# One step of a hybrid attention layer: the high parts of raw weights copied by GpSimd instead of VectorE

## The chip, the cores and the metric

The kernel runs on one core of one Trainium2 chip. A core has five engines with queues of their own, each working in order: TensorE (PE in the profile, its weight loads PEld), VectorE (DVE), ScalarE (ACT), GpSimd (POOL) and SyncE (SP), which here issues all DMAs. The metric is the device time of one execution in microseconds (us). The 1% of this time is about 12 us.

## The reference, cut to what matters

The layer projects a prompt of 2048 tokens (and 8 sample tokens) of width 1024, runs two kinds of attention over it, gates the outputs and projects them back:

```python
h = einsum('bsd,de->bse', x, w_in)
qa, ka, va, ga, qb, kb, vb, gb = split(h)          # rotary on qa, ka, qb, kb
oa = merge of three banded attentions of 8 heads (dilations 1, 4, 16)
ob = banded attention of 8 heads on 2 KV heads, with a learned sink per head
mix = concatenate([oa * silu(ga), ob * silu(gb)])
y = layer_norm(2**0.25 * x + einsum('bse,ed->bsd', mix, w_o))
```

Everything is float32 at the interface.

## The kernel before, in words

A float32 product with accuracy near float32 is made of three products in the faster type float32r: every operand is split into a **high part** (the value rounded to float32r) and a **low part** (value minus high part), and high x high, high x low and low x high are accumulated (`products`, and the same pattern at lines 629 and 672). So every weight tile needs two preparations after its load: a copy into the high part and a subtraction for the low part.

The kernel has three stages. In the first (up to about 381 us of the profile) the K and the A-side Q projections and V are made. In the last (from about 1059 us) the output projection and the normalisation run. Between them lies the steady stage: a loop over 66 steps of attention (`scores`, `weights`, `turn`, `values`; 12 steps for each pair of A heads, then 4 for each pair of B heads), in which TensorE also does the later projections. Those come from a generator (`stream`, `out_weights`) that is advanced by a budget of 3480 ns per step, each of its 256-column products counting n/2.4 ns. In this stage the order of the instructions on every engine is that of the program (a manual schedule): nothing is reordered.

The later projections go in three passes over eight chunks of tokens: QB0, QB1, QB2, G0 in the first pass, G1 to G4 in the second, G5 to G7 in the third. All weights of a pass are replaced at the change to the next: the tiles gw0, gw1 (shown as gw), gw2 and gw3 are reopened as the last chunk has used them. TensorE's products of a projection are shown as pg at line 629.

How these weights arrive is the part around the change. `Parts` puts four raw chunks of a weight (128 x 256 float32 each) into the queue `raws`. At every tick of the loop (four per step) `raw_step` does two things. It takes up to two chunks from the head of the queue whose load was issued at least three ticks ago and whose destination is open, and issues for each a copy into the high part h (line 137) and a subtraction into the low part l on GpSimd (line 138). Then it issues up to two loads (line 142, on SP) into the four buffers named raw. A buffer is free again when the subtraction has read it. 17 weights take this way, 68 chunks: two of the first pass (the other two were prepared before), four of the second, three of the third, and the eight blocks of the output weights (shown as wo, wo6h, wo7h and wl).

Other work on the same queues: on VectorE the mask and row minimum of the scores (line 831, sm), the copies of transposed probabilities out of PSUM (line 859, pT), the regrouping of queries (line 800, qo), the transposed statistics (line 930, stT) and the gates (line 172, th); TensorE's transposes (line 853, ps_pt) and scores (line 823, ps_s) wait for these. On GpSimd the weighting of the three A patterns (`merge_a`, lines 1050 to 1053), whose factors F come by DMA, and the merges of the B pairs (line 990). `merge_a` fetches F two chunks ahead on SP (line 1038), and a fetch waits for the buffer that GpSimd still reads.

Of the kernel before, what the change touches and what calls it, by code (L numbers as in the profile page):

```python
# [51 lines left out]
def hymba_step(ctx, tc, xt, xs, xr, wq, wv, wo, tab, msk, ident, diag, sinks, lng, lnb,  # L52
               kca, vca, kcb, vcb, y, kto, vo):
    nc = tc.nc
    V, S, G, T = nc.vector, nc.scalar, nc.gpsimd, nc.tensor
# [37 lines left out]
    def tick(last=False):  # L93
        slot[0] += 1
        raw_step()
        while due and (last or any(d.at <= slot[0] for d in due)):
            now = [d for d in due if last or d.at <= slot[0]]
            due[:] = [d for d in due if d not in now]
            for d in now:
                d.run()  # L100
# [13 lines left out]
    class Parts:  # L114
# [9 lines left out]
        def __iter__(self):  # L124
            while self.left:
                raw_step(True)
            return iter(self.hl)

    def raw_step(now=False):

        for r in raws:
            r[4] += r[3] is not None
        for _ in range(2):
            if raws and raws[0][0].hl and raws[0][3] is not None and (now or raws[0][4] >= 3):
                p, _, k0, w, _ = raws.popleft()
                h, l = p.hl
                V.tensor_copy(h[:, k0:k0 + 2], w)
                G.tensor_sub(l[:, k0:k0 + 2], w, h[:, k0:k0 + 2].bitcast(F32))
                p.left -= 1
        for r in [r for r in islice(raws, RAW) if r[3] is None][:2]:  # L140
            r[3] = at.tile([128, 2, 128], F32, name="raw", bufs=RAW)
            dma(r[3], r[1][:, r[2]:r[2] + 2])
# [1193 lines left out]
```

## Time and profile before

| what | value |
|---|---|
| median of 3 runs | 1244.24 us (1241.34 to 1249.01) |
| profiled execution | 1243.91 us, span 1242.1 us |
| mean granted TensorE clock | 0.978 of full |
| PE busy | 1149.4 us (93%) |
| DVE busy | 566.0 us (46%) |
| ACT busy | 430.9 us (35%) |
| POOL busy | 328.6 us (26%) |
| DMA | 230.15 MB, mean 185 GB/s |

In rows of the timeline the columns are start in us, duration in us, engine, line of the kernel, operation, output <- inputs, shapes, count; in brackets stands how long the engine was idle just before and what ended that. In rows of a line or tile the numbers behind the count are the shortest, median and longest duration in ns, then the first and last start. In rows of groups they are the busy time and the mean duration, then the idle time just before and its releasers. In rows of waits stand the total in us and the number of times. "EVENT_SEMAPHORE" and the names with a q are the sequencers. A merged row covers several instructions.

### The profile page before, as it was taken

To read this page: it belongs to the slowest core of one execution; us is meant where nothing else is said; L and a number is where in the kernel's file an instruction comes from. 1 tells how busy PE (TensorE), PEld (TensorE's weight loads), DVE (VectorE), ACT (ScalarE), POOL (GpSimd) and SP (SyncE) were. 2 spreads that over 40 slices of the span, in tenths; PEclk is the share of its full clock that TensorE was granted. 3 is DMA by queue.
4 is the path that set the end of the run, shared out by engine and by line. 5 is a ranking of instruction groups with operands and counts; after the bars stand their busy time and mean duration, and the time that the engine had idled before them with its cause. 6 is when DMAs were issued, how large, how long until landed. Compare 5 with 4: busy or idle time off the path is not lost.

```text
span 1242.1 us, 23436 instructions
## 1 busy us (share of the span) xinstructions
PE 1149.4 (93%) x8614; PEld 1006.3 (81%) x8614; DVE 566.0 (46%) x1855; ACT 430.9 (35%) x1417; POOL 328.6 (26%) x402
## 2 busy tenths in 40 slices
PE   8999999999998999995999899779899896999997
PEld 7899999979977888984887788668777774688885
DVE  6432001010023565553666546465666774685434
ACT  3200111101103565552555445435554451133221
POOL 2243112120012000045105302540243323175432
PEclk9999999999999999997999999989999997999998
DMA  8745887283686573677466746854896847655621
GB/s 276 240 134 177 256 277 254 81 272 128 213 259 192 180 188 124 156 187 170 143 153 176 217 144 172 199 147 142 204 226 197 273 145 219 180 168 185 199 94 68
DMA packets 206067, 230.15 MB, mean 185 GB/s; under 512 B 34640, under 2 KB 174576, under 8 KB 205568
## 3 DMA queue, kind: packets, MB, share of 16 engines
q1 hardware_dynamic: 205952, 228.66, 63.2%
q8 instruction: 67, 1.10, 0.4%
q14 instruction: 48, 0.39, 0.1%
HBM read 158.52 MB, written 70.07 MB: 184 GB/s over the span
## 4 chain that ended last, share of the span: by engine, by line
PE 65%; DMA 13%; DVE 7%; ACT 5%; issue 4%; POOL 3%; SPq 2%; POOLq 0%; DVEq 0%; ACTq 0%
PE po L672 13%; PE pg L629 11%; PE ps_s L823 7%; PE pv L527 7%; PE ps_pt L853 5%; PE pmm L152 5%; PE ps L152 5%; PE ppt L152 4%; ACT pe L834 4%; PE ps_o L874 4%; DMA F<-fd 4%; PE po L152 3%; DVE pT L859 3%; DVE sm L831 2%; DMA k<-ks 2%
## 5 line engine op out<-in xcount | busy, mean ns | idle before, releaser
L834 ACT ACTIVATE pe<-sm,st 128x256 f32<-128x256 f32 (+1 forms) x512 | 235.6, 461 | 241.4 <-DVE st L831 240.4
L831 DVE CUSTOM_DVE_ANT_0 sm<-ps_s,mk 128x256 f32<-128x256 f32 (+1 forms) x512 | 180.4, 375 | 143.2 <-PE ps_s L823 132.5
L853 PE MATMUL ps_pt<-idt,pe 128*128 128x128 f32 x848 | 140.3, 286 | 48.5 <-DVE pT L859 37.6
L629 PE MATMUL pg<-gx,gw 128*128 128x256 f32 (+1 forms) x1104 | 167.5, 294 | 5.9 <-DMA gx<-xd 2.9
L853 PEld LDWEIGHTS ps_pt<-idt,pe 128*128 128x128 f32 x848 | 90.7, 141 | 73.3 <-DVE pT L859 48.9
L629 PEld LDWEIGHTS pg<-gx,gw 128*128 128x128 f32 x1104 | 142.7, 192 | 7.5 <-DMA gx<-xd 3.5
L859 DVE COPY pT<-ps_pt 128x512 f32<-128x512 f32 x176 | 121.2, 689 | 28.3 <-PE ps_pt L853 26.4
L1050 POOL TENSOR_TENSOR oT<-oT,F 128x256 f32<-128x256 f32 x32 | 23.4, 731 | 347.3 <-ACT pe L834 179.4
L874 PE MATMUL ps_o<-pT,v 128*64 128x128 f32 (+1 forms) x1120 | 106.0, 333 | 0.0
L874 PEld LDWEIGHTS ps_o<-pT,v 128*64 128x64 f32 x1120 | 69.7, 136 | 39.3 <-issue 16.6
L834 ACT ACTIVATION_READ_ACCUMULATOR pe<-sm,st 128x1 f32 x512 | 95.8, 187 | 0.0
L823 PE MATMUL ps_s<-k,qo 64*128 64x256 f32 (+1 forms) x768 | 95.5, 390 | 0.0
L823 PEld LDWEIGHTS ps_s<-k,qo 64*128 64x128 f32 x768 | 69.3, 195 | 13.4 <-issue 1.8
L629 PE MATMUL pg<-gx,gw2h 128*128 128x256 f32 (+1 forms) x368 | 75.1, 292 | 1.2 <-ACT spe L406 1.2
L527 PE MATMUL pv<-wvh,xh 128*128 128x384 f32 (+1 forms) x224 | 69.6, 311 | 0.0
L527 PE MATMUL pv<-wvh,xl 128*128 128x384 f32 (+1 forms) x224 | 69.5, 310 | 0.0
L527 PE MATMUL pv<-wvl,xh 128*128 128x384 f32 (+1 forms) x224 | 69.4, 310 | 0.0
L672 PE MATMUL po<-wl,mho 128*128 128x512 f32 x192 | 59.7, 392 | 0.0
L629 PEld LDWEIGHTS pg<-gx,gw2h 128*128 128x128 f32 x368 | 58.3, 191 | 1.5 <-ACT spe L406 1.5
L629 PE MATMUL pg<-gx,gw2l 128*128 128x256 f32 (+1 forms) x184 | 53.9, 293 | 0.0
L539 ACT ACTIVATE vf<-pv 128x384 f32<-128x384 f32 (+1 forms) x32 | 14.0, 438 | 112.7 <-PE pv L527 62.2
L172 DVE SCALAR_TENSOR_TENSOR th<-th,pg 128x256 f32<-128x256 f32 (+1 forms) x64 | 26.9, 420 | 48.7 <-ACT th L168 48.3
(262 smaller groups left out, 2461.8 us busy)
## 6 DMA issues: line engine op xcount, KB each, us to landing
gx<-xd SPq DMA_DIRECT2D x80, 512.0 KB
F<-fd SPq DMA_DIRECT2D x80, 192.0 KB
gs<-th SPq DMA_DIRECT2D x64, 128.0 KB
v<-vs SPq DMA_DIRECT2D x28, 256.0 KB
xd<-xh SPq DMA_DIRECT2D x12, 512.0 KB
xd<-xl SPq DMA_DIRECT2D x12, 512.0 KB
kc<-in_kca SPq DMA_DIRECT2D x8, 768.0 KB
vc<-in_vca SPq DMA_DIRECT2D x6, 1024.0 KB
```

The lines of the kernel that those rows point to most:

```text
L152: T.matmul(p[:, :n], a[:, kt, :], b, start=k == 0, stop=k == 23)
L172: V.scalar_tensor_tensor(th[:, :n], th[:, :n], 1.0, p, op0=OP.add, op1=OP.mult)
L527: T.matmul(p[:, :w], l, r[:, kt, :w], start=k == 0, stop=k == 23)
L629: T.matmul(p[:, :n], a[:, kt, :], b[:, kt % 2, :n], start=kt + e == 0, stop=kt == 7 and e == 2)
L672: T.matmul(p, a, b[:, nh * 4:nh * 4 + 4].rearrange("p a b -> p (a b)"), start=first and k == 0, stop=last and k == end)
L823: T.matmul(s[:, h, n % 4, :w], self.Q[g][r, n % 4 * 128:n % 4 * 128 + 128], self.keys(n)[r], start=True, stop=True)
L831: V.tensor_tensor_reduce(sm[:, :w], self.s[:, h, n % 4, :w], mk[:, MI[self.d], 256 - w:], -0.125, 3.0e38, op0=OP.add, op1=OP.min, accum_out=m)
L834: S.activation(p[:, :w], sm[:, :w], AF.Exp, scale=-1.0, bias=m, accum_out=den)
L853: T.transpose(pt[:, h, j], self.P[h, n][:, a:a + 128], idt)
L859: V.tensor_copy(t, pt)
L874: T.matmul(o[64 * h:64 * h + 64, a:a + 128 * len(ns)], v[:, cv, kv:kv + 64], t[:, h, j:j + len(ns)].rearrange("p a b -> p (a b)"), start=n ...
L1050: G.tensor_mul(m, m, F[:, 0])
```

## The change

The copy into the high part in `raw_step` is issued on GpSimd instead of VectorE. The subtraction that follows it stays on GpSimd, and so do the loads on SP, the buffers, the order of the queue `raws` and all other code.

```diff
             if raws and raws[0][0].hl and raws[0][3] is not None and (now or raws[0][4] >= 3):
                 p, _, k0, w, _ = raws.popleft()
                 h, l = p.hl
-                V.tensor_copy(h[:, k0:k0 + 2], w)
+                G.tensor_copy(h[:, k0:k0 + 2], w)
                 G.tensor_sub(l[:, k0:k0 + 2], w, h[:, k0:k0 + 2].bitcast(F32))
                 p.left -= 1
```

## The prediction

> **What bounds the kernel now.** I read the page first: the share of each engine, then the chain that ended last.
>
> ```profile
> span 1242.1 us, 23436 instructions
> PE 1149.4 (93%) x8614; PEld 1006.3 (81%) x8614; DVE 566.0 (46%) x1855; ACT 430.9 (35%) x1417; POOL 328.6 (26%) x402
> PE 65%; DMA 13%; DVE 7%; ACT 5%; issue 4%; POOL 3%; SPq 2%; POOLq 0%; DVEq 0%; ACTq 0%
> ```
>
> TensorE bounds the kernel, so only time in which it stands still can be won: 1242.1 - 1149.4 = 93 us. VectorE (DVE) has over half the span free, so relieving it of busy time means little; what counts is where it stands in front of something TensorE needs. So the second view is line 137, the copy that the change moves, and what it waits for.
>
> ```profile
>   DMA raw<-in_wq: 28.6, 8
>   DMA raw<-in_wo: 5.0, 3
>   POOL gw2l L138: 27.2, 5
> ```
>
> VectorE stood 28.6 + 5.0 = 33.6 us waiting for raw weights in eleven places. The third row is the other direction: GpSimd (POOL) waited 27.2 us for copies that VectorE had not reached yet. Third, the timeline shows whether TensorE stood still in these places. The first is the change from the first to the second pass of the projections.
>
> ```profile
> 569.46 1.89 SPq L142 DMA_DIRECT2D raw<-in_wq  x4
> 575.37 1.96 DVE L137 CAST gw<-raw 128x256 fp32r<-128x256 f32 x4 [13.18 <-DMA raw<-in_wq]
> 577.58 1.12 PE L853 MATMUL ps_pt<-idt,pe 128*128 128x128 f32 x4 [10.25 <-DVE stT L930]
> 578.68 2.80 POOL L138 TENSOR_TENSOR gw<-raw,gw 128x256 fp32r<-128x256 f32 x4
> 585.23 0.64 DVE L137 CAST gw<-raw 128x256 fp32r<-128x256 f32 x2 [2.55 <-DMA raw<-in_wq]
> 586.53 0.44 PE L853 MATMUL ps_pt<-idt,pe 128*128 128x128 f32 x2 [2.78 <-DVE pT L859]
> 588.28 3.15 PE L823 MATMUL ps_s<-k,qo 64*128 64x256 f32 x16
> 597.19 0.63 PE L629 MATMUL pg<-gx,gw 128*128 128x256 f32 x4
> 599.71 2.00 PE L823 MATMUL ps_s<-k,qo 64*128 64x256 f32 x16
> ```
>
> VectorE's queue came to the copy at 562.2 us, 7 us before the load was even issued. The attention's copies (stT, then sm and pT) stood behind it, and TensorE behind these: 10.25 and 2.78 us. The weights were not needed yet: the second pass begins at 597.19. The second place is the next change of pass, the third the loads of the output weights before the last stage.
>
> ```profile
> 807.95 0.64 DVE L137 CAST gw<-raw 128x256 fp32r<-128x256 f32 x2 [7.25 <-DMA raw<-in_wq]
> 809.24 1.12 PE L853 MATMUL ps_pt<-idt,pe 128*128 128x128 f32 x4 [7.19 <-DVE pT L859]
> 812.45 1.43 DVE L137 CAST gw<-raw 128x256 fp32r<-128x256 f32 x2 [2.59 <-DMA raw<-in_wq]
> 814.54 0.44 PE L853 MATMUL ps_pt<-idt,pe 128*128 128x128 f32 x2 [2.43 <-DVE pT L859]
> 815.88 3.68 PE L823 MATMUL ps_s<-k,qo 64*128 64x256 f32 x16
> 816.13 2.77 POOL L138 TENSOR_TENSOR gw<-raw,gw 128x256 fp32r<-128x256 f32 x4
> 834.69 1.23 PE L629 MATMUL pg<-gx,gw 128*128 128x264 f32 x8
> ```
>
> ```profile
> 1041.21 0.69 DVE L137 CAST wo7h<-raw 128x256 fp32r<-128x256 f32 x2 [2.45 <-DMA raw<-in_wo]
> 1043.98 0.37 PE L963 MATMUL pst<-idt,wts 128*32 128x128 f32 x1 [4.65 <-DVE wts L959]
> 1080.45 144.14 PE po L672 x622
> ```
>
> The last row is the chain of waits: after these places TensorE runs through, so what is won before arrives at the end.
>
> **The change part by part.** 68 copies (17 weights in four chunks each) go from VectorE to GpSimd, each directly ahead of the subtraction of the same chunk. Loads, their order on SP, buffers and subtractions stay.
>
> *Removed, first change of pass:* TensorE's waits of 10.25 + 2.78 = 13.0 us go. What could be late next: the q and v of the coming steps.
>
> ```profile
> 563.32 1.19 SPq L782 DMA_DIRECT2D v<-vs  x2
> 579.13 1.08 SPq L906 DMA_DIRECT2D q<-qa  x2
> ```
>
> These are the last issues of either. The v is wanted by the values of the step that now begins at 588.28, the q two steps later; with some 6 us to land, neither is late for a TensorE 13 us earlier.
>
> *Removed, second change:* 7.19 + 2.43 = 9.6 us. *Removed, tail:* 4.65 us; the seven small VectorE operations of the merge no longer stand behind wo7h.
>
> *Slow clock behind the stalls.*
>
> ```profile
> 540.00:562.00 22.00, 22.00 (x190) 19.30 (x189) 13.99 (x51) 13.77 (x51) 9.25 (x13) 1.00 0.90 237
> 562.00:578.00 16.00, 5.75 (x49) 4.38 (x48) 2.77 (x9) 0.49 (x2) 8.92 (x14) 0.76 0.84 171
> ```
>
> These are windows before and in the first stall (engines in the order PE, PEld, DVE, ACT, POOL; then the granted clock, 1.00 against 0.76, the DMA engines' share and GB/s). Sixteen scores take 2.00 us at 599.71, but 3.15 at 588.28 and 3.68 at 815.88: 1.15 + 1.68 = 2.8 us. Transposes and products around them run at the same clock (TensorE was busy only 5.75 us of the 16); I estimate about as much again for them, 5 us in all.
>
> *Removed from VectorE's queue:* busy time.
>
> ```profile
> 381.00:1034.00 653.00, 22.44 (x64) 0.98 0.66 179
> L138 POOL TENSOR_TENSOR gw<-raw,gw 128x256 fp32r<-128x256 f32 x16 | 11.5, 742 | 8.7 <-DVE gw L137 4.5 <-DMA raw<-in_wq 4.2
> L174 POOL COPY sgS<-th 128x8 f32<-128x8 f32 x8 | 1.5, 190 | 30.7 <-DVE th L172 30.7
> L365 POOL MEMSET z<- 128x1088 f32 x1 | 1.0, 1007 | 20.7 <-PE ppt L152 20.7
> L365 POOL MEMSET z<- 128x256 f32 x1 | 0.3, 312 | 0.0
> L110 POOL TENSOR_TENSOR mlp<-mtp,mhp 128x256 fp32r<-128x256 f32 x16 | 14.9, 932 | 24.8 <-ACT mhp L109 24.7
> ```
>
> The window holds 64 copies of 22.44 us. Most lie where VectorE waits for TensorE or ScalarE anyway; some stand ahead of a pT that TensorE waits for. Between 0 and 10 us; I take 2, since the waits that I counted hold the large ones.
>
> *Added to GpSimd:* the trace has no such copy on GpSimd. From below a memset of the same size, 0.31 us; from above the slowest two-input group of this size, 0.93, the usual one being 0.74. The copy of 8 elements takes 0.19, and the memsets grow by (1007 - 312)/832 = 0.84 ns per element: 0.19 + 248 x 0.84 ns = 0.40 us, the value I take, nearest to the memset. In all 68 x 0.40 = 27 us on an engine that is busy 26%.
>
> *The added wait.* GpSimd now stands for the raw load itself. Behind it stand the merge's multiplications and the subtractions, but it stood there before too, for VectorE, which stood for the same load. So no new wait, only 0.40 us more per chunk. Are the weights in time for a TensorE 13 us earlier? The second pass would begin at 597.19 - 13.0 = 584.2. A step of attention takes 599.71 - 588.28 = 11.4 us and brings 32.6 products (3480 ns at 256/2.4 ns each in the code); a weight with 24 products is used up in 8.4 us. So the four weights are wanted at 584.2, 592.6, 601.0 and 609.4. GpSimd starts the first at 578.7 (the merge stands before it) and needs 4 x (0.40 + 0.74) = 4.6 us: 583.3. There are four raw buffers; the next load waits for a subtraction, takes 5.9 us (569.46 to 575.37), and its last two chunks need 2.3 us: 8.2 us per weight, hence 591.5, 599.7, 607.9. In time by one or two us, so little slack. At the second change: wanted at 834.69 - 9.6 - 2.6 (clock) = 822.5, ready at 816.13 + 4.6 = 820.7. With 0.74 for the copy each weight adds about 1.3 us, 3 to 4 us per change of pass; I take 1.5 for each of the two, 3 us. At the start of the first pass the same two effects cancel (nothing counted).
>
> **Sum:** 13.0 + 9.6 + 4.65 + 5 + 2 - 3 = 31 us. The profiled execution took 1243.91 us, 1.8 more than its span and 0.3 below the median of 1244.24, so the two agree: 1243.9 - 31 = **1213 us**.
>
> [...] The row first:
>
> ```profile
> 1041.68 1.49 POOL L138 TENSOR_TENSOR wo7l<-raw,wo7h 128x256 fp32r<-128x256 f32 x2 [0.23 <-DVE wo7h L137]
> 1041.82 0.71 DVE L956 TENSOR_TENSOR dn<-wts,st 128x32 f32<-128x32 f32 x1
> 944.76 0.19 DVE L956 TENSOR_TENSOR dn<-wts,st 128x32 f32<-128x32 f32 x1
> ```
>
> The same small operation takes 0.71 us while GpSimd subtracts and 0.19 elsewhere. The Trainium skill (SBUF — State Buffer, Who interferes with whom) says that VectorE and GpSimd share one pair of SBUF ports, held for a whole instruction, and that copies in a two-port mode and operations with two SBUF inputs are shut out meanwhile; the trace agrees with these 0.71 against 0.19 us. [...]
>
> **The rivals.** *1. The weights become the wait.* The slack above is one or two us per weight. If a load takes 8 us instead of 5.9 (all DMA engines are at 0.84 to 0.90 in the windows above), each of the three later weights of a pass slips by 2 us: 6 us for each change of pass, 12 in all: 1225 us. For it: the second weight's loads also stand in SP's queue behind the merge. Against: the loads are released earlier where GpSimd waited for VectorE (27.2 us).
>
> *2. Slower: the copy itself is slow on GpSimd.* Place: the nine weights that are loaded while TensorE is near them (two at the start, four, three). Price: at most 4 x (c - 0.40) us each, 36 x (c - 0.40) in all. The gain is eaten at c = 1.26 us, and from c = 1.6 us it is slower by over 1%; at 1.7 us, 1213 + 47 = 1260 us. For it: no row shows a copy to this type on GpSimd. Against: it would be over twice the two-input time.
>
> *3. Nothing is left: the ports.* Each of 68 copies shuts VectorE out for 0.40 us where it needs the pair: at most 27 us, 1240 us. For it: the rows of line 956. Against:
>
> ```profile
> L831 DVE CUSTOM_DVE_ANT_0 sm<-ps_s,mk x512: 280/416/427, 386.4 to 1019.6; 128x256 f32<-128x256 f32 x112, 128x128 f32<-128x128 f32 x59
> L859 DVE COPY pT<-ps_pt x176: 676/691/694, 396.1 to 1028.9; 128x512 f32<-128x512 f32 x176
> ```
>
> The mask operation and the copy out of PSUM, which make up the path (shortest, median and longest time in ns), are never longer than 0.43 and 0.70 us, whether GpSimd runs or not; and VectorE's own copies drop out.
>
> *4. The stalls stay,* because something else holds VectorE there: 1244. Against: the copies behind it (stT) had their input from TensorE 13 us earlier.
>
> **How the numbers follow.** Forecast 0.62 (1203 to 1221), first rival 0.18, second 0.06, third 0.10, fourth 0.04. About 1%, 12 us, is what can be told from no change, so faster means below 1232: 0.62 + 0.18 = 0.80; same 0.14; slower 0.06. The range leaves out the second and fourth rivals and part of the third: from 1201 (VectorE's relief 8 us more and no lateness) to 1236.
>
> **What would show it.** In the changed kernel, line 137 is on GpSimd with about 0.40 us each; no wait for raw on VectorE; no wait of 10.25 or 7.19 us of TensorE at the changes of pass, granted clock near 1.00 there; the second pass starts some 13 us earlier, the last stage some 30. Wrong would be: TensorE's products waiting for gw by over 5 us per change; copies over 0.75 us; or loads of v, q or gx as the new wait of TensorE.

## The result and the profile after

The changed kernel takes 1210.04 us (median of 4 runs, 1207.77 to 1211.41), the kernel before 1243.97 in the same job (4 runs). The ratio is 0.9721 with a 95% interval of 0.9686 to 0.9755: 34 us faster, where 31 were forecast. The profiled execution took 1207.77 us with a span of 1206.0, so the two traces differ by 36.1 us of span. First the head of the page of the changed kernel, then the rows of line 137 (shortest, median and longest copy, first and last start; idle time of its engine and number of times):

```profile
span 1206.0 us, 23406 instructions
PE 1139.4 (94%) x8614; PEld 997.6 (83%) x8614; DVE 549.5 (46%) x1787; ACT 430.9 (36%) x1417; POOL 353.3 (29%) x470
```

```profile
L137 POOL CAST gw<-raw x16: 394/400/597, 575.3 to 805.8; 128x256 fp32r<-128x256 f32 x16
  DMA raw<-in_wq: 18.6, 5
  DMA raw<-in_wo: 8.5, 5
```

The copies run on GpSimd at 0.40 us. GpSimd now waits 27.1 us for raw weights; VectorE waited 33.6 for them before. The wait is nearly as long, but on an engine that TensorE's next work doesn't depend on. TensorE is busy for 1139.4 us instead of 1149.4 with the same 8614 products.

Where the time came from is read by cutting both traces at the same instructions (the first score product of a step; the first cut lies 3.6 us behind one, where VectorE had reached its wait) and asking for the busy time of each engine in each stretch. In each pair the first row is before, the second after; the columns are the window and its length, busy time and instructions of PE, PEld, DVE, ACT and POOL, the granted clock, the DMA share and GB/s. The stretches are the first change of pass, the second, the third pass up to the last step's scores, and the end:

```profile
567.20:599.70 32.50, 18.78 (x131) 15.98 (x127) 16.59 (x56) 11.30 (x39) 16.56 (x23) 0.79 0.61 151
563.90:580.20 16.30, 15.78 (x129) 13.60 (x129) 10.45 (x35) 10.24 (x36) 11.75 (x18) 1.00 0.84 202
795.60:829.00 33.40, 21.94 (x157) 17.98 (x156) 15.71 (x54) 10.87 (x39) 18.69 (x30) 0.85 0.68 169
775.10:793.60 18.50, 18.50 (x159) 15.75 (x158) 12.07 (x44) 10.89 (x39) 9.91 (x15) 1.00 0.60 148
829.00:1013.10 184.10, 168.59 (x1450) 141.84 (x1448) 120.40 (x444) 95.83 (x337) 51.26 (x74) 1.00 0.70 198
793.60:982.70 189.10, 169.40 (x1447) 141.98 (x1446) 117.06 (x423) 95.85 (x337) 75.26 (x122) 1.00 0.76 208
1013.10:1242.10 229.00, 207.95 (x974) 162.06 (x973) 121.97 (x237) 55.19 (x98) 97.70 (x93) 0.96 0.50 157
982.70:1206.00 223.30, 204.45 (x974) 159.48 (x973) 120.09 (x222) 55.13 (x98) 96.69 (x102) 0.98 0.51 159
```

Length minus PE busy is the time in which TensorE stands still. From these rows:

| stretch | shorter by | of it standing still | of it quicker products |
|---|---|---|---|
| up to the first change | 567.2 - 563.9 = 3.3 | (not cut further) | |
| first change of pass | 16.2 | 13.72 - 0.52 = 13.2 | 3.0 |
| second pass between the changes | 195.9 - 194.9 = 1.0 | | |
| second change of pass | 14.9 | 11.46 - 0 = 11.5 | 3.4 |
| third pass | -5.0 | 15.51 - 19.70 = -4.2 | -0.8 |
| the end | 5.7 | 21.05 - 18.85 = 2.2 | 3.5 |
| sum | 36.1 | | |

The product counts of a pair differ by up to three (131 and 129, 157 and 159), so a few tenths of a us in the last column are not certain. The timeline shows the same places as the prediction's fences did; in the changed kernel TensorE waits in none of them, except at line 629 for gx:

```profile
570.15 2.00 PE L823 MATMUL ps_s<-k,qo 64*128 64x256 f32 x16
577.90 0.63 PE L629 MATMUL pg<-gx,gw 128*128 128x256 f32 x4
784.13 2.00 PE L823 MATMUL ps_s<-k,qo 64*128 64x256 f32 x16
819.61 2.02 SPq L581 DMA_DIRECT2D gx<-xd  x4
823.73 0.98 PE L629 MATMUL pg<-gx,gw 128*128 128x256 f32 x6 [1.42 <-DMA gx<-xd]
827.05 0.62 PE L629 MATMUL pg<-gx,gw 128*128 128x256 f32 x3 [0.64 <-DMA gx<-xd]
1006.74 0.27 PE L963 MATMUL pst<-idt,wts 128*32 128x128 f32 x1
```

The scores of the two changes of pass take 2.00 us instead of 3.15 and 3.68. The product at line 963 waits for nothing. New is a wait at the start of the third pass: the pieces of x (gx) are issued at 819.61, behind the loads of v and the stores of the gates on SP, and TensorE, which comes 35 us earlier than before at the end of the second change, stands for them. (Two waits for gx in the second pass, 0.54 and 2.40 us, were there before the change too; after it they are 0.80 and 1.37 us.)

### The profile page after: what moved, and what is told of

Read it like the earlier page. It is cut to its first block, busy times and chain, and to the rows that moved or that the text cites. A ratio compares the mean times of both kernels' runs of the same rounds, so it can differ in the third digit from the quotient of the medians.

```text
span 1206.0 us, 23406 instructions
## 1 busy us (share of the span) xinstructions
PE 1139.4 (94%) x8614; PEld 997.6 (83%) x8614; DVE 549.5 (46%) x1787; ACT 430.9 (36%) x1417; POOL 353.3 (29%) x470
## 4 chain that ended last, share of the span: by engine, by line
PE 71%; DMA 12%; DVE 6%; ACT 5%; issue 3%; POOL 2%; SPq 2%; DVEq 0%; POOLq 0%; ACTq 0%
PE po L672 13%; PE pg L629 12%; PE pv L527 8%; PE ps_s L823 7%; PE ps_pt L853 6%; PE ps_o L874 5%; PE ppt L152 5%; PE pmm L152 5%; PE ps L152 5%; ACT pe L834 3%; DMA gx<-xd 3%; PE po L152 3%; DMA F<-fd 3%; DVE pT L859 2%; DVE sm L831 1%
## 5 line engine op out<-in xcount | busy, mean ns | idle before, releaser
L859 DVE COPY pT<-ps_pt 128x512 f32<-128x512 f32 x176 | 121.2, 689 | 32.7 <-PE ps_pt L853 30.6
L823 PE MATMUL ps_s<-k,qo 64*128 64x256 f32 (+1 forms) x768 | 92.7, 381 | 0.0
```

Of the source, the lines that this page charges most:

```text
L823: T.matmul(s[:, h, n % 4, :w], self.Q[g][r, n % 4 * 128:n % 4 * 128 + 128], self.keys(n)[r], start=True, stop=True)
L859: V.tensor_copy(t, pt)
```

## The experiments

Three theories were put to the test. **A**: the price was VectorE's place in the queue; it stood at the head for a load, and the attention's copies stood behind it. **B**: the price was VectorE's busy time, and the ports that it shares with GpSimd. **C**: the weights are ready sooner, or GpSimd and SP are no longer held up by VectorE. Ratios are to the kernel before, on the same chip, with 95% intervals.

**1 and 2. Half of the change each.** In one kernel only the projection weights are copied by GpSimd, in the other only the output weights. The diff is against the kernel before and shows only the lines that differ; its comments say which kernel has which line.

```diff
-            self.hl, self.left = hl, 4
+            self.hl, self.left, self.wq = hl, 4, src.tensor is wq.tensor
-                V.tensor_copy(h[:, k0:k0 + 2], w)
+                (G if p.wq else V).tensor_copy(h[:, k0:k0 + 2], w)   # first kernel
+                (V if p.wq else G).tensor_copy(h[:, k0:k0 + 2], w)   # second kernel
```

> The copies of the 36 chunks of projection weights are on GpSimd, those of the 32 chunks of output weights are back on VectorE. Theory A (VectorE's queue stood for raw loads; the price is TensorE's wait behind it): both changes of pass keep their gain, only the 5 to 6 us of the tail come back: 1215 us, with a wait of TensorE of 4 to 5 us for line 959 as before. Theory B (VectorE's busy time and the ports): 36 of 68 copies give about half of the 34 us: 1226 us. Theory C (weights ready earlier, GpSimd and SP no longer held up by VectorE): 1212 us, as the output weights are not late.

> The opposite half: the 32 chunks of output weights on GpSimd, the 36 of projection weights on VectorE. Theory A: only the tail is won, 5 to 6 us: 1238 us, with the waits of 10 and 7 us at the changes of pass as before. Theory B: 32 of 68 copies, about half: 1228 us. Theory C: nothing, 1244 us.

Measured: 1211.46 us, ratio 0.9754 (0.9729 to 0.9779), and 1236.24 us, ratio 0.9948 (0.9928 to 0.9969). The losses of ratio, 0.0246 and 0.0052, add up to 0.0298, and the whole change has 0.0279. Each half brings what its own stalls cost: in the first kernel the wait of the end is back (the waits: total, times, longest), in the second kernel the timeline has the stall of the first change of pass again.

```profile
PE pst L963 <- DVE wts L959: 6.4, 1, 6.4
```

```profile
572.61 1.96 DVE L137 CAST gw<-raw 128x256 fp32r<-128x256 f32 x4 [12.88 <-DMA raw<-in_wq]
574.82 1.12 PE L853 MATMUL ps_pt<-idt,pe 128*128 128x128 f32 x4 [9.94 <-DVE stT L930]
```

The second kernel takes 32 of the 68 copies off VectorE, about half of the busy time, and wins about 6 us of 34: the gain goes with the stalls, not with the copies.

The first kernel alone doesn't separate A from C: A had forecast 1215 us, and the 1211.46 measured is the number of C (1212). Its trace agrees with A all the same. The end stage, cut as above, takes 229.1 us there, as in the kernel before (229.0), and 223.1 in the second kernel, as in the changed kernel (223.3). By the spans of the traces the first kernel is 4.3 us slower than the changed one (1210.3 against 1206.0), by the medians 1.4.

**3. VectorE's busy time given back.** Beside each copy on GpSimd, VectorE copies a tile of the same size (the mask, onto itself), which waits for no load. The output is unchanged.

```diff
                 G.tensor_copy(h[:, k0:k0 + 2], w)
+                V.tensor_copy(mk[:, 0], mk[:, 0])
```

> The changed kernel, and beside every GpSimd copy a copy of the same size on VectorE at the same place, from the mask tile onto itself (mk, 128x256), which waits for no load: the busy time and the use of the ports are back, the wait is not. Theory A: 0 to 4 us slower than the changed kernel, 1210 to 1214 us. Theory B: the gain goes, 1240 us. Theory C: as A.

Measured: 1212.95 us, ratio 0.9770 (0.9736 to 0.9804), inside A's range. Its group of added copies and its waits:

```profile
L138 DVE COPY mk<-mk 128x256 f32<-128x256 f32 x68 | 32.7, 481 | 1.4
PE ps_pt L854 <- DVE pT L860: 27.8, 42, 1.2
```

VectorE has 32.7 us more to do, 0.48 us for a copy on average (median 0.36, longest 1.80), and the kernel keeps the gain to within 3 us, which the intervals don't tell from nothing. No wait for pT is above 1.2 us. This speaks against B.

**4. The copies on ScalarE.** VectorE is relieved as fully as by the change, but the wait goes to another engine that the attention needs.

```diff
-                G.tensor_copy(h[:, k0:k0 + 2], w)
+                S.activation(h[:, k0:k0 + 2], w, AF.Copy)
```

> The copies are on ScalarE, not on GpSimd or VectorE. Theory A: ScalarE has a queue in order and the exponentials of the attention stand in it, so the same loads hold up TensorE through the exponentials: 1236 to 1246 us, with stalls of TensorE at the two changes of pass. Theory B: VectorE is relieved, ScalarE is busy 36%: 1212 us. Theory C: 1225 to 1240 us, as GpSimd waits for ScalarE instead of VectorE.

Measured: 1245.06 us, ratio 1.0017 (0.9994 to 1.0039): the whole gain is gone. Timeline of the first change of pass, then ScalarE's idle time before line 137 for the projection weights:

```profile
578.30 0.77 ACT L137 ACTIVATE gw<-raw 128x256 fp32r<-128x256 f32 x2 [12.48 <-DMA raw<-in_wq]
579.40 0.42 PE L928 MATMUL pst<-idt,st 128*64 128x128 f32 x1 [11.84 <-ACT pT L857]
  DMA raw<-in_wq: 28.6, 8
```

The same 28.6 us in eight places, now at the head of ScalarE's queue, and TensorE stands behind ScalarE's pT as it stood behind VectorE's. B would have had 1212 here, C 1225 to 1240. So it is not the relief of VectorE alone that wins.

**5. The kernel before, with only the first weight's copies later.** All copies stay on VectorE. Only the first weight of the second and of the third pass is taken from the queue nine ticks after its load's issue instead of three. The diff shows only the lines that differ, and its comment isn't in the code.

```diff
-            self.hl, self.left = hl, 4
+            self.hl, self.left, self.age = hl, 4, 3
-            if raws and raws[0][0].hl and raws[0][3] is not None and (now or raws[0][4] >= 3):
+            if raws and raws[0][0].hl and raws[0][3] is not None and (now or raws[0][4] >= raws[0][0].age):
+                            ws[more[0]].age = 9   # it stays 3 for all others
```

> The kernel before, all copies on VectorE; only the copies of the first weight of the second and of the third pass stand later in VectorE's queue (at nine ticks after their load instead of three or four, about 12 us). Theory A: the waits of 13 us and 7 us go or shrink, since the load has landed when the queue comes to the copy; the next weight's loads are issued later in exchange and may hold VectorE 2 to 4 us each: 1217 to 1230 us. Theory B: busy time and ports are unchanged: 1244 us. Theory C: the weights are made later still, so 1244 us or slower.

Measured: 1222.82 us, ratio 0.9824 (0.9772 to 0.9876). With GpSimd and VectorE doing just what they did before, 21 of the 34 us are won by the place of the copies alone. VectorE's idle time before line 137, its first copy, and two of TensorE's waits:

```profile
  DMA raw<-in_wq: 8.3, 6
577.91 1.15 DVE L137 CAST gw<-raw 128x256 fp32r<-128x256 f32 x2 [4.42 <-DMA raw<-in_wq]
582.15 0.89 PE L854 MATMUL ps_pt<-idt,pe 128*128 128x128 f32 x4 [2.08 <-DVE pT L860]
PE pst L964 <- DVE wts L960: 5.7, 1, 5.7
```

8.3 us instead of 28.6, and the stall of the first change of pass falls from 10.25 to 2.08 us, the longest of the second from 7.19 to 3.06; that of the end, where nothing was edited, stays, and the end stage takes 230.4 us. The copies for the change of pass start later here than in the kernel before (577.91 against 575.37 us), which speaks against C.

**6. Every copy on GpSimd twice.** It asks how much later the weights may be.

```diff
                 G.tensor_copy(h[:, k0:k0 + 2], w)
+                G.tensor_copy(h[:, k0:k0 + 2], w)
```

> The changed kernel with every GpSimd copy issued twice (the second writes the same values): 0.80 us per chunk instead of 0.40 plus 0.73 for the subtraction. This measures the slack of the weights, which the prediction put at one or two us per weight and charged with 3 us. If that holds, 4 x 0.4 = 1.6 us per weight makes TensorE wait 3 to 8 us in all: 1213 to 1218 us. If there is much more slack, 1210 to 1211 us. If GpSimd's time is the price of the change, 68 x 0.4 = 27 us: 1237 us.

Measured: 1216.55 us, ratio 0.9776 (0.9738 to 0.9815). The time lies in the range that was given to a small slack of the weights, but mostly for another reason, so the range was met in part by luck. At the changes of pass no product waits for a weight. Weights are late only at the start of the first pass: TensorE waits four times for gw3, 1.2 us in all, and the first two steps of the loop are 2.0 us longer together than in the changed kernel. The largest loss in one step, 5.2 us, is a wait for x. TensorE's timeline, and SP's issue of the last piece that it waits for, in this kernel and then in the changed kernel:

```profile
659.81 0.33 SPq L582 DMA_DIRECT2D gx<-xd  x1
666.72 1.65 PE L630 MATMUL pg<-gx,gw 128*128 128x256 f32 x6 [3.54 <-DMA gx<-xd]
```

```profile
652.23 0.33 SPq L581 DMA_DIRECT2D gx<-xd  x1
```

The piece is issued 7.6 us later. The step in which it is issued begins some 4 us later here too, so SP has lost about 4 us to TensorE. SP's waits for the buffers of F, which GpSimd reads, are no longer in total than in the changed kernel (19.9 against 20.1 us). What is longer is SP's wait, ahead of the loads of F, until the store of the factors (fd) has landed (this kernel, then the changed one):

```profile
SPq L1039 <- DMA fd<-wts: 8.0, 2, 5.9
```

```profile
SPq L1038 <- DMA fd<-wts: 4.6, 2, 2.4
```

The longest of these waits is 3.5 us longer, about what SP has lost, and the loads of F behind it are issued at 631.72 us instead of 624.43, already 7.3 us late, some 25 us ahead of the piece. It is once more an instruction that waits for a transfer at the head of a queue, with a load that TensorE needs behind it. Whether the second copies made that store land later stays open. What the run settles is that 68 more copies, 27 us of GpSimd, cost about 6 us between the medians, and none of it through weights at the changes of pass.

**7 and 8. The pieces of x earlier.** The wait for gx at the start of the third pass is the price that the changed kernel still pays. In the seventh kernel the loads of the next chunk's x are issued beside the first weight of a chunk instead of the second, in all chunks. The comments in the diff say which kernel has which line.

```diff
-                            if c2 is not None and kt % 2 == 0 and i == 1:
+                            if c2 is not None and kt % 2 == 0 and i == 0:   # seventh
+                            if c2 is not None and kt % 2 == 0 and i == (0 if pi == 1 or (pi == 2 and c == route[0]) else 1):   # eighth
```

> The changed kernel with the loads of the next chunk's activations (gx) issued during the first weight's products of a chunk instead of the second's. In the changed kernel TensorE waits for gx at the start of the third pass's second chunk, and 3 us of the gain are lost between two neighbouring steps there. If SP's lateness with these loads is the cause, 2 to 4 us are won: 1206 to 1208 us, and the wait for gx shrinks below 2 us in all. If the DMA engines are the limit, 1210 us.

Measured: 1211.34 us, ratio 0.9741 (0.9699 to 0.9783), no gain: the expectation was missed. The waits for gx are gone (and SP's wait for the store of fd is 0.8 us instead of 4.6), and two others have come, one at the first chunk, one late in the third pass:

```profile
391.51 0.78 PE L629 MATMUL pg<-x,gw2h 128*128 128x264 f32 x2 [5.27 <-ACT qf L182]
943.48 1.11 PE L853 MATMUL ps_pt<-idt,pe 128*128 128x128 f32 x4 [4.11 <-DVE pT L859]
```

The eighth kernel keeps the earlier loads only where they had won (second pass, first chunk of the third).

> The changed kernel, with the x pieces (gx) of the next chunk loaded one weight earlier only in the second pass and in the first chunk of the third: the three places where loading all of them earlier won 3.0, 1.9 and 3.1 us, without the two places where it lost 4.8 and 4.9 us. If the three gains stand by themselves: 1210 - 8 = 1202 us, range 1200 to 1205, and TensorE's waits of 0.3 to 1.7 us for gx at the start of the third pass are gone. If an earlier load on SP only passes the wait on to another load (or the buffers come around so that the loss at the later step of the third pass stays): 1207 to 1211, with a wait of 3 to 5 us at a new place.

Measured: 1202.73 us (1195.95 to 1207.23, 6 runs), ratio 0.9660 (0.9624 to 0.9696). It has the lowest time of all; its interval touches that of the changed kernel (0.9686 to 0.9755), so how much it wins over that (7 us between the medians, 3.8 between the two traces' spans of 1202.2 and 1206.0 us) is less certain than the 40 us over the kernel before in the same job. The timelines show the three gains one by one, first in the changed kernel, then in the eighth:

```profile
689.57 0.97 PE L629 MATMUL pg<-gx,gw 128*128 128x256 f32 x6 [0.80 <-DMA gx<-xd]
691.91 0.79 PE L629 MATMUL pg<-gx,gw 128*128 128x256 f32 x2 [1.37 <-DMA gx<-xd]
692.63 3.79 PE L823 MATMUL ps_s<-k,qo 64*128 64x256 f32 x16
705.57 1.16 PE L823 MATMUL ps_s<-k,q 64*128 64x128 f32 x16
827.71 2.00 PE L823 MATMUL ps_s<-k,qo 64*128 64x256 f32 x16
```

```profile
692.08 2.00 PE L823 MATMUL ps_s<-k,qo 64*128 64x256 f32 x16
703.09 1.16 PE L823 MATMUL ps_s<-k,q 64*128 64x128 f32 x16
822.84 2.00 PE L823 MATMUL ps_s<-k,qo 64*128 64x256 f32 x16
```

The eighth kernel's trace began its attention 2.3 us later and was 2.4 us behind in the step before 692; at 692.08 it is 0.5 ahead, a step later 2.5 (703.09 against 705.57; its scores at 692 take 2.00 us instead of 3.79), and at 822.84 4.9, where it was 1.8 ahead a step earlier: 3.0 + 1.9 + 3.1 = 8.0 us. So the three gains are seen in the trace; how much of them is left at the end is not settled: of a lead of 6.5 us ahead of the end stage, 2.7 are lost in that stage, where nothing was edited.

## Why the prediction was right, point by point

- **What bounds it, and the mechanism.** Held. The four waits that were counted (10.25, 2.78, 7.19 and 2.43 us at the changes of pass) and that of the end are gone, and 4 and 5 show that it was the place in the queue: the same wait on ScalarE wins nothing, and later copies on VectorE win 21 us.
- **First change, 13.0 us.** TensorE stands still 13.2 us less.
- **Second change, 9.6 us.** 11.5 us less; small waits beside the two counted ones went too.
- **Slow clock, 5 us.** Mis-sized: 3.0 + 3.4 = 6.4 us of quicker products at the two changes, and another 3.5 in the end, which the prediction left out (granted clock there 0.96 before, 0.98 after). Whether these 3.5 belong to the change is not shown: see the last section.
- **The end, 4.65 us.** Over-sized. The wait is gone, but TensorE stands still only 2.2 us less. Part of it came back as waits for the high part hh of an input of the output projection, which ScalarE writes (before, then after):

```profile
PE po L672 <- ACT hh L109: 4.4, 2, 2.3
```

```profile
PE po L672 <- ACT hh L109: 6.7, 3, 3.4
```

- **VectorE's busy time, 2 us.** Not seen: between the changes of pass, in the second pass, where no counted stall lies, the stretch is 1.0 us shorter, and giving 32.7 us back costs at most 3. Nothing and 2 us can't be told apart.
- **The copy, 0.40 us.** Held: median 0.400. The Trainium skill (GPSIMD Engine Reference, Engine selection) gives a factor of about two for GpSimd against VectorE for operations with two inputs, and calls one input roughly line-rate. The measured 0.40 us against VectorE's mean of 0.35 (22.44 / 64) is a factor of 1.14, against its median of 0.29 one of 1.4; both lie nearer to the latter.
- **Lateness of the weights, -3 us.** The step that failed, by name and cause. At the changes of pass no product waited for a weight, and none over 0.3 us elsewhere by TensorE's waits. (At the start of the first pass TensorE's weight load ahead of a product is put down to gw2 with 2.27 us; the product itself stood there for 2.09 us for ScalarE's qf, and for 2.17 before the change: the rows are below.) The working asked for a whole weight before its first product, and for 5.9 us per load:

```profile
576.98 1.07 SPq L142 DMA_DIRECT2D raw<-in_wq  x2
577.63 0.60 POOL L137 CAST gw<-raw 128x256 fp32r<-128x256 f32 x1
581.44 0.40 POOL L137 CAST gw<-raw 128x256 fp32r<-128x256 f32 x1 [1.24 <-DMA raw<-in_wq]
PE pg L629 <- POOL gw3l L138: 0.5, 2, 0.3
```

The pass begins at 577.90, while the third of the four chunks is still being copied: a product waits for its chunk alone. And the next load landed 4.5 us after its issue (581.44 - 576.98). What was lost instead, about as much, was lost to x: the third pass is 5.0 us longer, 3.1 of it in the step of the gx wait, and another 1.1 in its last step (see the ports below). The prediction had named gx among the new waits that would make it wrong, and had no price for it.
- **Start of the first pass, 0.** 3.3 us came before the first change. 1.7 of them lie ahead of the first step (380.9 against 379.2), where no moved copy has run yet; they belong to the execution, not to the change: the ten traces begin that step anywhere from 377.1 to 381.5 us. The other 1.6 came in the first steps, where a wait of 1.68 us for the last weight's high part, which VectorE copied late, is gone (before, then after):

```profile
390.28 0.51 PE L629 MATMUL pg<-x,gw2h 128*128 128x264 f32 x2 [2.17 <-ACT qf L182]
397.32 0.48 PE L629 MATMUL pg<-x,gw3h 128*128 128x264 f32 x2 [1.68 <-DVE gw3h L137]
```

```profile
388.48 0.48 PE L629 MATMUL pg<-x,gw2h 128*128 128x264 f32 x2 [2.09 <-ACT qf L182]
```

The two effects that were to cancel didn't quite.
- **The rivals.** *Weights as the wait* didn't come at the changes of pass, even with every copy twice (6). *Slow copy* didn't, at 0.40 us. *Ports*: 3 shows that the gain doesn't hang on them, though VectorE does stand for GpSimd: its copies in 3, issued beside copies of GpSimd, take 0.28 us at the shortest and 0.48 on average. This agrees with the Trainium skill (SBUF — State Buffer, Who interferes with whom), by which the shared pair of ports is held for whole instructions. Mostly it cost VectorE time that it had to spare. In one place it cost TensorE about 1.1 us, in the last step of the third pass (before, then after):

```profile
1010.59 0.19 DVE L953 TENSOR_TENSOR wts<-mn,snk 128x32 f32<-128x32 f32 x1
```

```profile
979.25 0.79 POOL L138 TENSOR_TENSOR wo<-raw,wo 128x256 fp32r<-128x256 f32 x1
979.36 0.73 DVE L953 TENSOR_TENSOR wts<-mn,snk 128x32 f32<-128x32 f32 x1
980.75 0.66 PE L853 MATMUL ps_pt<-idt,pe 128*128 128x128 f32 x4 [0.84 <-DVE pT L859]
```

The small operation takes 0.73 us beside GpSimd's subtraction instead of 0.19, and the pT that TensorE waits for stands right behind it. The subtraction ran on GpSimd before the change too, but later in the step (at 1013.07 us), behind a copy that stood in VectorE's queue after this operation (1012.65). This step takes 10.8 to 11.1 us in the six kernels in which GpSimd copies the output weights and 10.0 in the four in which it doesn't. So the third rival had the right ports; its size, 27 us for the copies, was far off.

The mechanism was right; that the sum came out so near is in part luck, since its errors partly compensate: the standing still at the changes was 24.7 us (13.2 + 11.5) against 22.6, the clock 9.9 against 5, the end 2.2 against 4.65, and the loss 5.0 in another place than the 3 expected.

## What to carry to other kernels

Ask of every instruction that waits for a load which engine stands at the head of its queue for it, and what stands behind it there; move it to an engine whose next work is not wanted, or later in its queue, and don't ask first which engine does it fastest. The busy share of the engine that was relieved told nothing about the gain here: 46% before and after, and 34 us won. After such a change look again at the queue that issues the loads, since the bound engine comes to everything earlier: in this kernel that won 8.0 us in three steps of the trace (7 us between the medians, with intervals that touch), 3.1 of them at a place that had become late only through the change.

## What the runs showed of the hardware

- A short stall can cost more than it lasts, but need not. In the changed kernel waits of 0.70, 0.80 and 1.37 us within five microseconds, the first for pT, are followed by sixteen scores of 3.79 us instead of 2.00, at a granted clock of 0.50 (window 692.60 to 696.50); taking the two gx waits away won 3.0 + 1.9 us. In the kernel before, the same scores take 3.79 us behind waits of 0.54 and 2.40. But behind the waits of 1.42, 0.28 and 0.64 us in the third pass the scores at 827.71 take 2.00 us, at a clock of 1.00. What decides between the two is not shown.
- The granted clock in the end stage, 229 us long, is 0.96 before and 0.98 after, with the same 974 products: 3.5 us. The other traces don't tie this to the change: TensorE is busy there for 204.2 to 208.4 us in the six kernels in which GpSimd copies the output weights, and for 207.1 to 208.0 in the three in which VectorE does. The length of the stage does differ: 223.1 to 227.5 us in the six, 229.0 to 230.4 in the three.
